# One denoising step of a hybrid backbone: residual kept in DRAM during the two networks, block products from the fifth pair on, some dots moved

## The chip, the cores and the metric

The kernel runs on one core of a Trainium2 chip. The core has a matrix engine (TensorE, "PE" in the profile; its weight loads are shown as "PEld"), a vector engine (VectorE, "DVE"), an activation engine (ScalarE, "ACT"), GpSimd ("POOL"), SyncE ("SP"), and 16 DMA engines that all issuing engines share. The metric is the device time of one execution in microseconds (us). The kernel before took 1848.61 us, the median of three runs from 1846.2 to 1849.77.

## The reference

One step of a backbone of two layers over 128 context tokens and 512 latent tokens, 1024 wide, all in float32:

```python
DEPTH = 2; D_MODEL = 1024; SEQ = 128; DEC_SEQ = 512; FFN_HIDDEN = 2816
for i in range(DEPTH):
    p_sh1, p_sc1, p_g1, p_sh2, p_sc2, p_g2 = modulation(c_ctx[None], mod_w[i], mod_b[i])
    s_sh1, s_sc1, s_g1, s_sh2, s_sc2, s_g2 = modulation(c, mod_w[i], mod_b[i])
    hp = modulate(xp, norm_mix_g[i], p_sh1, p_sc1)      # rmsnorm * (1 + scale) + shift
    hs = modulate(xs, norm_mix_g[i], s_sh1, s_sc1)
    op, os_ = mixer(hp), mixer(hs)                      # layer 0: two-way state scan; layer 1: attention
    xp = xp + p_g1 * op
    xs = xs + s_g1 * os_
    xp = xp + p_g2 * conv_ffn(modulate(xp, norm_ffn_g[i], p_sh2, p_sc2), *ffn_p)
    xs = xs + s_g2 * conv_ffn(modulate(xs, norm_ffn_g[i], s_sh2, s_sc2), *ffn_p)

def conv_ffn(h, up_w, conv_w, conv_b, down_w):
    u = dwconv(h @ up_w, conv_w, conv_b)                # 1024 -> 2 x 2816, width-3 convolution over tokens
    a, v = jnp.split(u, 2, axis=-1)
    return (jax.nn.silu(a) * v) @ down_w                # 2816 -> 1024

def modulation(cvec, w, b):
    m = jax.nn.silu(cvec) @ w + b                       # 1024 -> 6 x 1024
    return jnp.split(m[:, None, :], 6, axis=-1)
```

Each layer's `conv_ffn` is called a network here: the first network is that of layer 0, the second that of layer 1. The running `x` (640 tokens, 1024 wide) is the residual.

## The kernel before, in words

**Layout.** Features lie on the 128 partitions and all 640 tokens in the columns, so the residual is eight tiles of 128 x 640, `self.x[i]`. A float32 matrix product is made of three products of a faster format: every operand is split into a rounded part "hi" and the rest "lo", and hi·hi, hi·lo and lo·hi are added in PSUM. A block of 128 x 128 weights is so used three times, over two column ranges each (256 and 384, or 320 and 320): six matrix instructions.

**Stages.** The scan stage with its projection (`ssd`, L1131), the first network (`ffn`, L640, layer 0), the attention with its projection (`attention`, L1387), and the second network (`ffn`, layer 1). `stages` (L1496) and `run` (L1470) open and close memory pools around them.

**Order of the work.** The code is a straight list of instructions. A planner then sets the order on each engine from program order, readiness and an estimated cost of each instruction; every engine, and the queue of transfers that an engine issues, runs its list in that order. Side work is written as generators (`add`, L77): `hook` (L82), called after each weight block, advances a generator once as many ticks have passed as it asked for, and `drain` (L95) runs it to its end at that place of the program.

**Weights.** They come as "units" of up to 128 x 1024 in the order of use (`weight_units`, L1432). `prefetch` (L134) loads a unit from SP's queue into one of four "raw" slots. `cast` (L146) splits it: ACT writes hi, and lo is written either by DVE (raw - hi, L107) or, for the units in `self.summed`, by ACT (-hi) and an adding transfer of the weights from DRAM on POOL's queue (L181). `self.deep` says how many units ahead casts run (1, or 2 in the second network).

**The networks.** The 22 pairs of hidden tiles are made in stretches (`SUB`, L37), and after each stretch `project_out` (L321) multiplies the finished hidden tiles by the down weights, into eight output tiles. `gate_add` (L317) adds each PSUM result, times the gate, to the residual: DVE, three instructions per tile. The last stretch goes through `project_last` (L329), which also squares the new residual for the following norm. The first network has three stretches (8, 7, 7 pairs), the second five (4, 4, 4, 4, 6).

A pair in plain form is two tiles over eight weight blocks: 96 matrix instructions. From pair `S0[l]` on a pair is computed as a 2 x 2 block product with seven multiplications in place of eight, from sums of weights and sums of activations. `pair8` (L750), in the second network from pair 4, takes blocks of 4 + 4 weight blocks: 84 instructions of 320 columns. `pair7` (L782), in the first network from pair 16, takes 2 + 2 and does the remaining four plainly: 90. The sums of activations are made by `operands` (L688), those of weights in `cast`. `epilogue` (L657) does the convolution, SiLU and product on ACT and DVE, and splits the hidden tile; in the second network its lo is made by an adding transfer on POOL (L669). Both use the four slots "t" of 128 x 640 for temporary tiles.

**Memory.** The tag "f" has 19 slots of 128 x 640 for whatever is that size: the residual, scan inputs, raw tiles of the networks. The summed activations of the first network take over slots of the modulation work.

**Modulation of layer 1.** `mod_rest` (L598) makes 48 rows, each a 512 KB load and two dots (one for the latent tokens' vector, one for the context's) of 1024 columns on DVE (L620). All of it runs in the first network, as a generator that asks for 7 ticks, or 2 during a projection. It must end ahead of the stage that uses it.

**PSUM.** Up to the second network PSUM is a pool of three tiles of 1024 columns (`psd`); the second network uses six tiles of 512 (`psb`).

Of the kernel before, what the change touches and what calls it, by code (L numbers as in the profile page):

```python
# [18 lines left out]
P = 128  # L19
# [17 lines left out]
SUB = ((0, 8), (8, 15), (15, 22)), ((0, 4), (4, 8), (8, 12), (12, 16), (16, 22))  # L37
MIDS = 9, 6
# [3 lines left out]
NS = 2, 4  # L42
S0 = 16, 4
TH = T // 2
ATT_SPLIT = 6
NF = 19
# [3 lines left out]
class Step:  # L50


    def __init__(self, ctx, tc, a):
# [9 lines left out]
        self.down = False  # L63
# [7 lines left out]
        self.ph = pool("acts", 1)  # L71
        self.psb = None
# [42 lines left out]
    def slot(self, tag, name, dt=F32, cols=T, bufs=None, pool=None, rows=P):  # L115
        return (pool or self.ph).tile([rows, cols], dt, tag=tag, name=name, bufs=bufs)

# [203 lines left out]
    def project_out(self, h, ks, g, tiles=range(KT)):  # L321

        for i in tiles:
            ps = self.dense_ps("po")
            self.dense(ps, self.nextw(), ks, h)
            for hf in "AB":
                self.gate_add(i, ps, g, hf)

    def project_last(self, h, ks, g, nextnorm, ks_last=None, parts="AB"):  # L329
# [3 lines left out]
        for i in range(KT - 3):  # L333
# [6 lines left out]
            for hf in "AB":  # L340
                self.gate_add(i, ps, g, hf)
                self.norm_sq(i, hf)
        ks = ks_last or ks
        if self.modtask:
            self.drain(self.modtask)
        ws = [(self.dense_ps("po"), self.nextw(), i) for i in range(KT - 3, KT)]
        for hf in parts:
# [5 lines left out]
            self.normt[hf] = self.add(nextnorm(hf), 3)  # L353

# [85 lines left out]
    def first_tiles(self, h, pool):  # L440
# [70 lines left out]
        for i in range(KT):  # L511
            xi = self.slot("f", f"x{i}", bufs=NF)
# [85 lines left out]
    def mod_rest(self, l, t0, pool):  # L598


        nc, a = self.nc, self.a
        cb = pool.tile([P, 2, D], F32, tag="cbc", name="cbc", bufs=1)
        nc.sync.dma_start(cb, a["cbc"])
        for c in range(2):
            sb = self.pw.tile([P, 1024], F32, tag="raw", name="csil", bufs=RAW)
            self.act(sb, cb[:, c, :], AF.Tanh, scale=0.5)
            self.stt(cb[:, c, :], sb, 1.0, cb[:, c, :], ALU.add, ALU.mult)
            nc.vector.tensor_scalar(cb[:, c, :], cb[:, c, :], 0.5, None, ALU.mult)
        yield 4
        for t in range(t0 - 1, 48):  # L610
            if t < 47:
                nxt = pool.tile([P, 1024], F32, tag="mw", name="mw", bufs=2)
                nc.sync.dma_start(nxt, a["modT"][t + 1])
            if t < t0:
                w = nxt
                yield 8
                continue
            junk = self.slot("sq", "junk", BF16, cols=1024, bufs=1)
# [995 lines left out]
```

## Time and profile before

| | |
|---|---|
| median of three runs | 1848.61 us |
| profiled execution, its own time | 1847.95 us |
| its span, first to last instruction | 1846.2 us |
| granted TensorE clock, mean | 0.994 |
| instructions | 33204 |
| bytes moved | 230.28 MB |

The profile gives busy times by engine, a timeline in 40 slices, the DMA queues, the chain of work that ended last, and groups of instructions by source line (a helper's line, mostly: L101 any ACT instruction, L104 and L107 any DVE one, L110 any matrix product). Names such as `po<-mh,whi` are output and inputs: `up` the PSUM of the networks' pairs, `st` that of a stage's first three tiles, `po` that of a projection, `whi` and `wlo` the split weights, `mh` and `ml` the split hidden tile, `raw` a loaded unit, `uraw` a raw hidden tile, `xr` the residual, `mw` a modulation row, `ca`, `cv` the epilogue's temporary tiles. A group's row ends with its busy time, the mean of one in ns, and the idle time of the engine ahead of it with what ended it.

The execution runs through the stages in this order: the scan until about 480 us (its first projection is mixed with the scan's end), the scan's last projection to 559, the first network to about 1026, attention and its projections to about 1390, the second network to the end.

### The profile page before, as it was taken

The numbers are of one execution on the slowest core, as the hardware profiler recorded it, in microseconds if no ns is written. First come the engines' busy times: TensorE is split into PE (matmuls) and PEld (weight loads), VectorE is DVE, ScalarE is ACT, GpSimd is POOL, SyncE is SP. The second block draws the span as 40 slices with busy tenths as digits, with TensorE's granted clock in tenths as the row PEclk, the third lists the DMA queues.
The fourth block names the chain that finished last, engine by engine and source line by source line (L and its number), as shares of the span: only waits on it lengthen the run. The fifth ranks groups of instructions, "written<-read, shape, count | busy, mean of one in ns | idle before, by whom it ended". The sixth has DMA issues, their size and how long they took to land.

```text
span 1846.2 us, 33204 instructions
## 1 busy us (share of the span) xinstructions
PE 1802.7 (98%) x13070; PEld 1704.8 (92%) x13070; DVE 1490.5 (81%) x2969; ACT 1038.7 (56%) x1987; POOL 49.2 (3%) x60
## 2 busy tenths in 40 slices
PE   7999999999999999999999999999999999999997
PEld 5899999999989999999999988888899999999996
DVE  5689999999748999987585878777878877768784
ACT  3489686879326441343353556656636554746561
POOL 0000000000000000000000000000000010101110
PEclk9999999999999999999999999999999999999998
DMA  9844343445533556542122211211124445546451
GB/s 337 264 135 138 99 148 105 121 137 179 187 133 104 194 183 214 194 133 78 57 82 91 80 48 60 65 55 38 55 83 110 104 114 141 126 129 154 122 137 58
DMA packets 90051, 230.28 MB, mean 125 GB/s; under 512 B 10428, under 2 KB 17192, under 8 KB 89768
## 3 DMA queue, kind: packets, MB, share of 16 engines
q1 hardware_dynamic: 81256, 207.13, 34.8%
q0 software_dynamic: 8064, 20.52, 6.6%
q8 instruction: 102, 1.67, 0.4%
q10 hardware_dynamic: 576, 0.52, 0.1%
q14 instruction: 53, 0.43, 0.1%
HBM read 215.29 MB, written 5.96 MB: 120 GB/s over the span
## 4 chain that ended last, share of the span: by engine, by line
PE 86%; DVE 6%; ACT 3%; DMA 3%; issue 2%; SPq 0%; POOL 0%; DVEq 0%; POOLq 0%; ACTq 0%
PE up L110 27%; PE po L110 25%; PE z L110 6%; PE x L110 5%; PE st L110 5%; PE yp L110 3%; PE bc L110 3%; PE q L110 2%; PE k L110 1%; PE modrow L110 1%; PE sl L110 1%; ACT whi L101 1%; PE ov L110 1%; PE v L110 1%; ACT e L101 1%
## 5 line engine op out<-in xcount | busy, mean ns | idle before, releaser
L101 ACT ACTIVATE whi<-raw 128x1024 fp32r<-128x1024 f32 (+3 forms) x243 | 227.8, 939 | 277.3 <-PE po L110 167.4
L107 DVE TENSOR_TENSOR wlo<-raw,whi 128x1024 fp32r<-128x1024 f32 (+3 forms) x207 | 227.0, 1097 | 43.0 <-ACT whi L101 37.5
L104 DVE SCALAR_TENSOR_TENSOR xr<-po,mod,xr 128x256 f32<-128x256 f32 (+2 forms) x279 | 107.8, 432 | 108.9 <-PE po L110 108.8
L110 PE MATMUL po<-mh,whi 128*128 128x256 f32 (+1 forms) x704 | 166.9, 310 | 0.0
L110 PE MATMUL po<-ml,whi 128*128 128x256 f32 (+1 forms) x704 | 166.6, 309 | 0.0
L110 PE MATMUL po<-mh,wlo 128*128 128x256 f32 (+1 forms) x704 | 166.3, 309 | 0.0
L110 PE MATMUL up<-h01l,whi 128*128 128x256 f32 (+1 forms) x596 | 146.2, 308 | 0.0
L110 PE MATMUL up<-h01h,whi 128*128 128x256 f32 (+1 forms) x596 | 146.1, 310 | 0.1
L110 PE MATMUL up<-h01h,wlo 128*128 128x256 f32 (+1 forms) x596 | 145.6, 308 | 0.0
L110 PEld LDWEIGHTS po<-mh,whi 128*128 128x128 f32 x704 | 128.0, 188 | 0.7 <-ACT mh L101 0.5
L110 PEld LDWEIGHTS po<-ml,whi 128*128 128x128 f32 x704 | 128.2, 188 | 0.2 <-DVE ml L107 0.2
L110 PEld LDWEIGHTS po<-mh,wlo 128*128 128x128 f32 x704 | 128.2, 188 | 0.0
L110 PEld LDWEIGHTS up<-h01h,whi 128*128 128x128 f32 x596 | 108.9, 188 | 1.5 <-ACT uraw L101 1.1
L110 PEld LDWEIGHTS up<-h01l,whi 128*128 128x128 f32 x596 | 109.1, 188 | 0.0
L110 PEld LDWEIGHTS up<-h01h,wlo 128*128 128x128 f32 x596 | 109.0, 188 | 0.0
L110 PE MATMUL up<-h11h,whi 128*128 128x320 f32 (+1 forms) x368 | 107.3, 309 | 0.0
L110 PE MATMUL up<-h11l,whi 128*128 128x320 f32 (+1 forms) x368 | 107.2, 309 | 0.0
L110 PE MATMUL up<-h11h,wlo 128*128 128x320 f32 (+1 forms) x368 | 107.1, 309 | 0.0
L104 DVE SCALAR_TENSOR_TENSOR cv<-uraw,fcw,cv 128x511 f32<-128x511 f32 (+1 forms) x176 | 85.3, 545 | 14.8 <-ACT cv L101 14.8
L104 DVE SCALAR_TENSOR_TENSOR ca<-uraw,fcw,ca 128x127 f32<-128x127 f32 (+1 forms) x176 | 86.7, 545 | 8.8 <-ACT ca L101 7.5
L101 ACT ACTIVATE mh<-cv 128x640 fp32r<-128x640 f32 x44 | 32.5, 738 | 88.8 <-DVE cv L107 88.8
L101 ACT ACTIVATE whi<-s 128x512 fp32r<-128x512 f32 (+1 forms) x96 | 52.8, 571 | 52.2 <-DVE s L107 22.7
(531 smaller groups left out, 5074.4 us busy)
## 6 DMA issues: line engine op xcount, KB each, us to landing
raw<-in_w_up SPq DMA_DIRECT2D x88, 512.0 KB, 3.4
mw<-in_modT SPq DMA_DIRECT2D x48, 512.0 KB, 3.8
raw<-in_w_in SPq DMA_DIRECT2D x40, 512.0 KB, 5.5
rb<-rowd SPq DMA_DIRECT2D x40, 512.0 KB, 5.4
raw<-in_w_qkv SPq DMA_DIRECT2D x24, 512.0 KB, 3.3
mr<-in_mod SPq DMA_DIRECT2D x44, 256.0 KB, 5.2
wlo<-in_w_up POOLq DMA_DIRECT2D x17, 512.0 KB, 5.2
mp<-in_modp SPq DMA_DIRECT2D x32, 256.0 KB, 5.4
```

Source lines behind the costliest of these rows:

```text
L101: return self.nc.scalar.activation(out, in_, func, **k)
L104: return self.nc.vector.scalar_tensor_tensor(out, in0, s, in1, op0, op1)
L107: return self.nc.vector.tensor_tensor(out, a, b, op)
L110: return self.nc.tensor.matmul(out, lhsT, rhs, start=start, stop=stop, skip_group_check=more)
```

## The change

Seven things change together.

1. **Residual.** The residual gets a pool of its own (`xslot`, eight slots), which also serves the first eight scan inputs; "f" falls from 19 slots to 11. `project_last` of the scan and of the attention write each new residual tile to DRAM (`save`, SP). The pool is closed when a network has made its first tiles, and the sums of activations of that network take its place. `restore` opens it again ahead of the network's last projection and loads the eight tiles.
2. **Projections of the networks.** All but the last write gate times result into a tile y (ACT, three instructions per output tile), and a transfer on POOL's queue adds y to the residual in DRAM. y comes from the "t" slots in the first network, from three slots of its own in the second.
3. **First network like the second.** Five stretches, PSUM as `psb`, casts two units ahead, `pair8` from pair 4; `pair7` is removed.
4. **More adding transfers.** lo of hidden tiles in the first network; lo of most up weights of the first network; lo of ten of the sixteen units of the scan's output weights.
5. **Dots.** Rows 0 to 11 run in the scan's last projection, one dot every 2 ticks, with three row slots, and are drained ahead of its last three tiles. Rows 12 to 47 run in the first network, from 84 ticks after its start, one dot every 5 ticks.
6. **Pools.** The scan's pools are closed ahead of its last projection; PSUM pools are opened anew for each stage.
7. **Casts** run two units ahead in the scan's projections too.

```diff
-SUB = ((0, 8), (8, 15), (15, 22)), ((0, 4), (4, 8), (8, 12), (12, 16), (16, 22))
-MIDS = 9, 6
+SUB = (0, 4), (4, 8), (8, 12), (12, 16), (16, 22)
+MIDS = 6
-NS = 2, 4
-S0 = 16, 4
+NS = 4
+S0 = 4, 4
+EARLY = 12
-NF = 19
+NF = 11
+    def open_x(self):
+        self.xp = self.xctx.enter_context(self.tc.tile_pool(name="resid", bufs=1, side="right"))
+    def xslot(self, name):
+        return self.slot("x", name, bufs=KT, pool=self.xp)
+    def save(self, i):
+        if not self.xd:
+            self.xd = [self.dram.tile([P, T], F32, tag=f"xd{j}", name=f"xd{j}") for j in range(KT)]
+        self.nc.sync.dma_start(self.xd[i], self.x[i])
+    def restore(self):
+        self.open_x()
+        self.x = [self.xslot(f"xr{i}") for i in range(KT)]
+        for i in range(KT):
+            self.nc.sync.dma_start(self.x[i], self.xd[i])
...
+    def project_out(self, h, ks, g, tiles=range(KT), to=None):
...
+            y = to()
             for hf in "AB":
-                self.gate_add(i, ps, g, hf)
+                for a, b, c in COND[hf]:
+                    self.act(y[:, a:b], self.cols(ps, hf, a, b), AF.Copy, scale=g[:, i, c:c + 1])
+            self.nc.gpsimd.dma_start(self.xd[i], y, accum_op=ALU.add)
...
+            if save:
+                self.save(i)
         ks = ks_last or ks
-        if self.modtask:
-            self.drain(self.modtask)
+        for t in (self.modtask, *before):
+            if t:
+                self.drain(t)
...
+    def mod_rest(self, l, t0, t1, alloc, junk_, every):
...
-                yield 2 if self.down else 7
+                yield every
...
-            if l and p < FT - 1:
+            if p < FT - 1:
                 self.act(lo, cv, AF.Copy, scale=-1.0)
                 nc.gpsimd.dma_start(lo, cv, accum_op=ALU.add)
...
-        self.deep = 2 if l else 1
+        self.deep = 2
...
+        self.xctx.close()
+        with self.tc.tile_pool(name=f"sums{l}", bufs=1, side="right") as tp:
+            self.seven = self.add(operands(sevens, tp), 1)
+            for s, (k0, k1) in enumerate(SUB):
+                while done < min(k1 + 1, FT):
+                    pair(done, done + 1 < min(k1 + 1, FT))
+                    done += 1
+                if s < len(SUB) - 1:
+                    self.project_out(mid, range(k0, k1), self.gate(l, 1),
+                                     to=lambda: self.slot("y", "y", bufs=3, pool=pool) if l else self.tmp("y"))
+        if self.modtask:
+            self.drain(self.modtask)
+            self.modtask = None
+        self.restore()
+        self.project_last(mid, range(*SUB[-1]), self.gate(l, 1), nextnorm, parts="CD" if l else "AB")
...
+        self.deep = 2
         self.project_out(hy, range(8), self.gate(0, 0))
...
+        close()
+        self.open_mod()
+        with self.tc.tile_pool(name="po", bufs=1) as pool:
+            self.modtask = self.add(self.mod_rows(2, pool, 7))
+            row = lambda: pool.tile([P, 1024], F32, tag="ew", name="ew", bufs=3)
+            junk = lambda: self.slot("t", "junk", BF16, cols=1024, bufs=4)
+            early = self.add(self.mod_rest(1, 0, EARLY, row, junk, 2), 1)
+            self.project_last(hy, range(8), self.gate(0, 0), nextnorm, save=True, before=[early])
...
+        self.summed = (set(up) - set(up[:5]) - set(up[half:half + 5]) - after) | set(so[3:13])
...
+            self.modtask = self.add(self.mod_rest(1, EARLY, 48, self.mod_row, junk, 5), 84)
```

213 lines of the change are left out of this document (81 added, 132 removed).

## The prediction

> **What bounds the kernel now.** I read the page first, for the busy shares and the chain that ended last.
>
> ```profile
> span 1846.2 us, 33204 instructions
> PE 1802.7 (98%) x13070; PEld 1704.8 (92%) x13070; DVE 1490.5 (81%) x2969; ACT 1038.7 (56%) x1987; POOL 49.2 (3%) x60
> ...
> PE 86%; DVE 6%; ACT 3%; DMA 3%; issue 2%; SPq 0%; POOL 0%; DVEq 0%; POOLq 0%; ACTq 0%
> ```
>
> PE is busy for 98% of the span and carries 86% of the chain. So an edit gains only if it takes PE work away, and loses only if it makes PE wait. Second I cut the two networks into stretches. The columns are the stretch, its length, the busy time of PE, PEld, DVE, ACT and POOL, the granted clock, the DMA share and GB/s. The first five rows are the first network (products, projection, products, projection, products); the next five are the second network from its fifth tile on, in the same alternation; the last is the projection that ends the scan stage.
>
> ```profile
> 582.75:688.36 105.61, 105.61 (x722) 105.61 (x722) 105.44 (x181) 54.03 (x68) 0.00 (x0) 1.00 0.55 180
> 688.36:744.66 56.30, 56.30 (x386) 56.30 (x386) 55.92 (x100) 10.63 (x12) 0.00 (x0) 1.00 0.66 211
> 744.66:843.30 98.64, 98.64 (x675) 98.64 (x674) 86.44 (x149) 43.20 (x54) 0.00 (x0) 1.00 0.46 148
> 893.10:973.94 80.84, 80.75 (x542) 79.34 (x542) 66.42 (x133) 42.98 (x78) 0.00 (x0) 1.00 0.25 80
> ...
> 1412.79:1464.06 51.27, 49.48 (x327) 49.22 (x327) 43.27 (x83) 36.95 (x63) 8.00 (x9) 0.97 0.58 119
> 1464.06:1492.06 28.00, 28.00 (x195) 28.00 (x194) 20.50 (x44) 10.44 (x17) 1.73 (x2) 1.00 0.47 129
> 1492.06:1541.32 49.26, 49.26 (x339) 49.26 (x338) 37.86 (x71) 34.97 (x60) 7.87 (x9) 1.00 0.58 128
> 1541.32:1569.40 28.08, 28.08 (x195) 28.08 (x194) 20.61 (x44) 10.44 (x17) 1.74 (x2) 1.00 0.49 145
> 1569.40:1618.66 49.26, 49.26 (x339) 49.26 (x338) 37.74 (x71) 35.13 (x60) 7.87 (x9) 1.00 0.60 128
> 1723.86:1785.43 61.57, 61.57 (x422) 61.57 (x422) 49.60 (x91) 45.19 (x77) 10.46 (x12) 1.00 0.65 151
> 480.00:560.00 80.00, 80.00 (x585) 72.88 (x583) 47.15 (x96) 26.93 (x41) 0.00 (x0) 1.00 0.38 128
> ```
>
> In every one of them but the second network's opening, PE has no idle time worth naming. The chain gives the products' counts:
>
> ```profile
> 582.75 105.61 PE up L110 x720
> ...
> 744.66 98.63 PE up L110 x672
> ...
> 1492.06 49.26 PE up L110 x336
> 1541.32 28.08 PE po L110 x192
> ...
> 1785.43 6.25 PE po L110 x42
> ```
>
> 105.61/720, 98.63/672, 49.26/336 and 28.08/192 are all 146.6 ns a product (320 columns on average): the number of products is the time, in dense tiles and in block products alike.
>
> **The block products.** A dense pair is 2 tiles x 8 blocks x 3 terms x 2 halves = 96 products; pair7 has 90, pair8 has 84 (7 blocks of 4 x 3). The first network issues 16 dense pairs and 6 of pair7 now (2076), then 4 dense and 18 of pair8 (1896): 180 fewer, 26.4 us at 146.6 ns. I take the sum from whole stretches, since those hold the waits too. Now, from the fourth tile on: 105.61 + 98.64 + 80.84 = 285.1 us. The second network does exactly the work that the first will have: 51.27 (five dense tiles and the first pair8), three times 49.26 (four pair8 each) and 61.57 (five) = 260.6. Difference: 24.5 us less. This already holds the price of an early start: 324 products at 146.6 ns are 47.5 us of the 51.27, so building the summed operands beside the first epilogues costs 3.8 us of waiting. That wait is the bound from one side: without it the gain is 28.2 us. The projections keep 22 x 6 x 8 products however they are cut.
>
> **Dots.** 24 of the 96 dots move to the scan's projection; 72 stay.
>
> ```profile
> L620 DVE CUSTOM_DVE_ANT_0 mw<-mw,cbc 128x1024 f32<-128x1024 f32 x18 | 21.9, 1219 | 0.2
> ...
> L104 DVE SCALAR_TENSOR_TENSOR xr<-po,mod,xr 128x256 f32<-128x256 f32 x15 | 6.7, 479 | 6.3 <-PE po L110 6.3
> ...
> L104 DVE SCALAR_TENSOR_TENSOR xr<-po,mod,xr 128x128 f32<-128x128 f32 x7 | 2.4, 341 | 0.0
> ```
>
> 36 dots ran in the first stretch (this row and its twin), where the code's spacing of 7 ticks would have put about 14: the planner pulls them forward into every gap. That is why DVE stands at 105.44 of 105.61 there with PE unharmed, and why I charge dots only for what does not fit. After, four pairs and a projection take 49.3 + 28.1 = 77.4 us of PE. DVE owes 37.8 + 20.6, less the gate additions that go to ACT (6.7 + 2.4), plus 88 ticks' worth of dots (8.8 rows x 2 x 1.22 = 21.5): 70.8 of 77.4. It fits as a total. Within the products alone it would be 37.8 + 13.7 = 51.5 of 49.3; bound 0 to 2.2 us for each of some 4.5 stretches, and I take 0, because the full DVE above is the nearest row.
>
> In the scan's projection DVE is idle for 80.0 - 47.2 = 32.9 us, and gets back 5 x 1.22 from weight splits that become transfers: 39. It owes 24 x 1.22 = 29.3, and four instructions of that width for the SiLU, at most 4.9: 34. At 4 ticks a row, 8 rows fit the 40 ticks before the drain; 8 dots (9.8 us) are left ahead of the last three tiles' gate additions, on which the norm and the first network's start wait. Bound: 0 to 9.8. I take 2, since the idle time is there, but their rows must also arrive (next).
>
> **Transfers.** Shares and landings in a stretch of the second network, of the dot rows, and of the residual's load:
>
> ```profile
> q0 software_dynamic: 1403, 3.55, 42.6%
> q1 hardware_dynamic: 1185, 2.69, 17.1%
> ...
> mw<-in_modT SPq DMA_DIRECT2D x48, 512.0 KB, 3.8
> ...
> ml<-cv POOLq DMA_DIRECT2D x21, 320.0 KB, 4.2
> ...
> xr<-in_xT SPq DMA_DIRECT2D x8, 320.0 KB, 4.6
> ```
>
> In 49.3 us, accumulating transfers moved 3.55 MB in 21.0 us of the 16 engines (169 GB/s), plain ones 2.69 MB in 8.4 us (319 GB/s). The new y of 0.328 MB goes into DRAM with addition, which no row shows. At the plain rate it costs 1.03 us, at the accumulating rate 1.94; the destination is another memory, so twice that, 3.9, is my upper end. I take 1.94, the nearest operation. A projection of the second network then needs 0.49 x 28.1 = 13.8, plus 8 x 1.94 = 15.5: 29.3 of 28.1 us, with a stretch at 58% behind it to catch up. In the first network come 3.2 dot rows (0.524 MB at 319 GB/s, 1.64 us each): 34.5 of 28.1, 6.4 us too much; over the whole 77.4 us it is 28.6 + 13.8 + 15.5 + 14.5 = 72.4. So nothing is bound for good, but each of four projections runs a backlog of 6.4 us against buffers of four weight tiles and four "t" slots, 14 us of tiles. Bounds 0 and 25.6 in all; I take 6, because the densest row with PE full stands at 66% and this at 123%.
>
> In the scan's projection 0.38 x 80 = 30 us are used; 12 rows (19.7), the conditioning vectors (1.05 MB by the code, 3.3), eight saves (8.2) and five weight splits (5 x 0.524 MB at 169 GB/s, 15.5) make 77 of 80: this is the other ground of the 2 us above.
>
> **Smaller parts.** The y evacuations are 24 ACT instructions a projection in place of DVE's.
>
> ```profile
> 1400.83 0.37 ACT L101 ACTIVATE uraw<-st 128x256 f32<-128x256 f32 x1
> ...
> 1350.00 0.33 SPq L643 DMA_DIRECT2D fcw<-in_fcw  x1
> ...
> L669 POOL DMA_DIRECT2D ml<-cv x16: 864/867/885, 1513.6 to 1781.8; - x16
> ```
>
> 24 x 0.37 = 8.9 brings ACT from 10.4 to 19.3 of 28.1: hidden; three PSUM tiles cover a late one. POOL issues 8 more at 0.87 us in 28: hidden; while it waits for a y, the weight additions of the next products stand behind it, but the first weight after a projection is left to DVE. A y slot is held for 1.1 (ACT) + 0.9 + some 4.2 = 6.2 us; the second network's three slots give 10.5 us. SP's saves (0.33 us of issue each) make it wait for a gate addition, with weight loads behind; those were asked for four units earlier: 0. The reload before the last projection may start when the last summed operand is read, 24 products (3.5 us) before 1785.43; the first tile lands 4.9 us later, at 1786.9, and its gate addition is due 36 products after 1785.43, at 1790.7: hidden by 3.8 us, bound 0 to 1 a network. In the second network DVE was not the limit, so the additions taken from it gain nothing.
>
> **Sum.** The profiled execution took 1847.95 us (span 1846.2 and 1.75 around it), 0.7 under the median of 1848.61. 1847.95 - 24.5 + 6 + 2 = 1831.5, 1832 against the median.
>
> **Rivals.** *All of it hidden* (25%): backlogs stay in the buffers, and the first network's opening may even miss its 3.8 us. 1820 to 1827. For it: 99.8% DVE with PE full. Against: no stretch above has more than 66% of DMA. The Trainium skill, "DMA: Bandwidth & Descriptors", section on the anatomy of one SWDGE transfer, fits such a transfer as 2.0 us fixed plus bytes at 436 GB/s, so that a y would be an estimated 2.8 us of which 0.75 moves data; the first network's projection would then need 13.8 + 6.0 + 5.2 = 25.0 of 28.1, and this case would be the forecast. The rows here have 4.2 us for the same bytes into SBUF, so I do not follow it.
>
> *The additions into DRAM fill the DMA engines* (17%, the other side). Per 77.4 us the first network leaves 77.4 - 28.6 - 13.8 - 14.5 = 20.5 us for eight y, 2.6 each; the second 4.4 each. Every microsecond beyond 2.6 costs 32 us in four projections. At 3.4 us a y the gain of 24.5 is gone; that is where it decides. At my upper end of 3.9 it is 32 x 1.3 = 42: about 1866. For it: a read and a write of DRAM for each y, never seen here. Against: the adding row, 1.94. The same page, section "Issuing engines are not separate DMA queues", says that transfers from all issuers share the 16 engines and interleave; the window's 0.60 is indeed the sum of the two queues' 42.6% and 17.1%.
>
> *Dots in the way* (10%): the drained dots hold the norm before the first network for up to 9.8 us and the products lose 2.2 a stretch: 1831.5 + 7.8 + 4.5 x 2.2 = 1849 at worst, some 1841 in the middle. For it: DVE runs in order, and a dot whose row is late blocks it. Against: dots waited for a row 0.2 us in 18.
>
> *The change does not do what it says*, block products that wait at each block: excluded as far as 49.26 us for 336 products goes, with one difference, the dots between them; it is inside the case above.
>
> **Chances.** Forecast 48% (1827 to 1838), all hidden 25%, dots 10%, DRAM additions 17%. The range runs from 1819 to 1850, leaving out most of the last case. What this kernel's times can tell from no change is about 0.2%, 3.7 us. Faster 0.79, same 0.05, slower 0.16.
>
> **What would show it.** The first network's first tile starts now at
>
> ```profile
> 559.17 0.28 PE L110 MATMUL st<-h01h,whi 128*128 128x256 f32 x1
> ```
>
> Right: 180 fewer products in the first network, its stretches of four pair8 near 49.3 us and of five near 61.6, projections within 1 to 2 us of 28.1, a DMA share above 0.9 in them, a y landing in 5 to 8 us. Wrong: PE waiting for weights or for ACT's evacuation in the projections, y landings over 9 us, DVE idle on a dot's row, or more than the present 582.75 - 559.17 = 23.6 us from that tile's start to the end of the first three.

## The result, and the profile after

The changed kernel takes 1889.7 us (median of 4 runs, 1884.9 to 1890.6) against 1848.1: a ratio of 1.022 with a 95% interval of 1.020 to 1.024. It is slower by 41.6 us, where 16.5 us less were forecast. Its page begins, and gives the chain, so:

```profile
span 1887.5 us, 33747 instructions
...
PE 1796.7 (95%) x12890; PEld 1687.6 (89%) x12890; DVE 1470.3 (78%) x2919; ACT 1178.2 (62%) x2347; POOL 162.7 (9%) x190
...
PE 69%; DVE 14%; DMA 9%; ACT 5%; issue 4%; SPq 0%; POOL 0%; DVEq 0%; ACTq 0%; POOLq 0%
```

The 180 products are gone (13070 to 12890), but PE is busy for only 6 us less, where 180 products at 146.6 ns are 26: the mean granted clock fell from 0.994 to 0.984, and a product kept PE busy for 139.4 ns in the mean in place of 137.9. The span grew, PE's part of the chain fell from 86% to 69%, and that of DVE and DMA together rose from 9% to 23%: PE now waits. The timeline of the first three tiles of each stage gives the stages' starts (the last two numbers are the first and last start of a group). Before:

```profile
L110 PE MATMUL st<-h01h,whi x48: 276/332/386, 559.2 to 582.1; 128*128 128x256 f32 x24, 128*128 128x384 f32 x24
L110 PE MATMUL st<-h10h,whi x48: 274/334/386, 1025.6 to 1048.7; 128*128 128x256 f32 x24, 128*128 128x384 f32 x24
L110 PE MATMUL st<-h11h,whi x48: 280/334/386, 1390.1 to 1412.3; 128*128 128x256 f32 x24, 128*128 128x384 f32 x24
```

After:

```profile
L112 PE MATMUL st<-h01h,whi x48: 276/334/387, 587.1 to 609.5; 128*128 128x256 f32 x24, 128*128 128x384 f32 x24
L112 PE MATMUL st<-h10h,whi x48: 276/334/387, 1069.5 to 1091.6; 128*128 128x256 f32 x24, 128*128 128x384 f32 x24
L112 PE MATMUL st<-h11h,whi x48: 276/334/386, 1432.7 to 1455.1; 128*128 128x256 f32 x24, 128*128 128x384 f32 x24
```

The loss is in two places. The first network starts 27.9 us later (2 forecast), and takes 482.4 us in place of 466.4 (about 448 forecast: 24.5 less, 6 more). Attention and the second network are 1.3 us shorter each, less than these stages differ between kernels that leave them alone (below). 27.9 + 16.0 - 1.3 - 1.3 = 41.3, the difference of the spans.

**The scan's last projection.** Windows of it after the change (PE, PEld, DVE, ACT and POOL busy; granted clock, DMA share, GB/s):

```profile
500.00:520.00 20.00, 17.38 (x109) 12.10 (x108) 3.70 (x7) 5.66 (x7) 0.87 (x1) 1.00 1.03 331
520.00:540.00 20.00, 20.00 (x114) 13.35 (x113) 12.74 (x23) 2.86 (x5) 0.86 (x1) 1.00 1.04 380
540.00:560.00 20.00, 15.44 (x114) 13.92 (x112) 17.99 (x38) 5.10 (x9) 0.00 (x0) 0.99 0.67 237
560.00:570.00 10.00, 5.07 (x22) 4.77 (x22) 10.00 (x19) 0.00 (x0) 0.00 (x0) 0.50 0.62 200
```

and pieces of its chain (start, length, what; `ew` is a modulation row in this stage, `xr` a tile of the residual):

```profile
497.97 9.86 DMA mr<-in_mod
...
548.51 0.48 DVE xr L106
549.00 1.13 DVE ew L665
...
550.14 1.14 DVE junk L665
...
568.86 0.64 DVE ew L665
```

First the DMA engines are full for 40 us, with the loads of the projection's own modulation rows (mr) at their head. Their buffers are now in the pool that is opened in place of the scan's, so those loads could start only when the scan had ended: the first is issued at 494.5 us, against 446.6 in the kernel before. Then PE is half idle, while DVE works off 15 dots (14 of about 1.14 us on the chain and a part of the last, 16.7 us) between the gate additions (xr) on which the norm waits.

**The first network.** Three stretches of four pair8, the second and third projection between them (cut at whole microseconds), and waits of DVE, ACT and PE over the whole network (total us, times, longest; `s` is a sum of weights):

```profile
692.10:750.10 58.00, 51.40 (x330) 50.74 (x329) 52.60 (x100) 32.88 (x59) 8.91 (x11) 0.91 0.76 197
750.10:780.10 30.00, 29.32 (x197) 28.79 (x196) 23.39 (x42) 19.71 (x41) 7.86 (x9) 1.00 0.96 252
780.10:844.10 64.00, 51.36 (x328) 50.84 (x329) 53.33 (x99) 33.37 (x60) 8.71 (x10) 0.89 0.73 183
844.10:874.10 30.00, 29.35 (x202) 29.08 (x200) 24.68 (x46) 18.98 (x40) 7.83 (x9) 1.00 0.98 258
874.10:932.10 58.00, 52.23 (x331) 51.71 (x332) 45.91 (x86) 34.48 (x61) 8.73 (x10) 0.94 0.64 157
```

```profile
ACT whi L103 <- DVE s L109: 53.2, 19, 13.6
...
DVE junk L665 <- DMA mw<-in_modT: 32.3, 13, 4.7
...
PE up L112 <- ACT uraw L103: 15.6, 3, 11.6
...
PE up L112 <- DVE wlo L109: 9.1, 3, 4.4
```

The projections take 30 us, with PE busy for 29.3, at a DMA share of 0.96 to 0.98 (28.1 plus 1 to 2 were forecast); it is the products behind them that take 58, 64 and 58 us in place of 49.3. The chain from the end of a projection into the second of these stretches shows how:

```profile
766.72 10.21 DMA mw<-in_modT
...
776.95 1.23 DVE junk L665
...
779.96 7.97 DMA mw<-in_modT
...
787.95 1.22 DVE junk L665
...
790.48 6.25 DMA mw<-in_modT
...
796.75 1.22 DVE junk L665
...
797.99 0.62 DVE s L109
...
798.71 0.63 ACT whi L103
799.34 0.34 ACT uraw L103
...
799.72 0.64 PE up L112
```

A row's load waits for its slot, the row lands after 6 to 10 us, its dot runs, the next load starts. Behind the last dot on DVE stands the sum (s) that the next weight operand (whi) is made from; behind that operand on ACT stands the copy of a finished hidden tile out of PSUM (uraw); and for this copy PE waits, three times, for up to 11.6 us. The landings between 640 and 930 us, which holds the three cycles, from the window's DMA view (KB each, median us; `xd` is the residual in DRAM):

```profile
mw<-in_modT SPq DMA_DIRECT2D x32, 512.0 KB, 6.4
raw<-in_w_up SPq DMA_DIRECT2D x24, 512.0 KB, 7.1
xd<-y POOLq DMA_DIRECT2D x24, 320.0 KB, 8.2
```

### The profile page after: what moved, and what is told of

It is laid out like the page before. It is cut to its first block, busy times and chain, and to the rows that moved or that the text cites. A ratio compares the mean times of both kernels' runs of the same rounds, so it can differ in the third digit from the quotient of the medians.

```text
span 1887.5 us, 33747 instructions
## 1 busy us (share of the span) xinstructions
PE 1796.7 (95%) x12890; PEld 1687.6 (89%) x12890; DVE 1470.3 (78%) x2919; ACT 1178.2 (62%) x2347; POOL 162.7 (9%) x190
## 4 chain that ended last, share of the span: by engine, by line
PE 69%; DVE 14%; DMA 9%; ACT 5%; issue 4%; SPq 0%; POOL 0%; DVEq 0%; ACTq 0%; POOLq 0%
PE up L112 19%; PE po L112 17%; PE z L112 6%; PE x L112 5%; PE st L112 4%; DMA mw<-in_modT 3%; PE bc L112 3%; PE yp L112 3%; PE q L112 2%; DVE wlo L109 2%; ACT whi L103 2%; PE k L112 1%; PE modrow L112 1%; PE v L112 1%; DMA raw<-in_w_up 1%
## 5 line engine op out<-in xcount | busy, mean ns | idle before, releaser
L103 ACT ACTIVATE whi<-raw 128x1024 fp32r<-128x1024 f32 (+2 forms) x259 | 224.8, 869 | 196.6 <-PE po L112 103.8
L109 DVE TENSOR_TENSOR wlo<-raw,whi 128x1024 fp32r<-128x1024 f32 (+2 forms) x178 | 176.7, 993 | 53.3 <-ACT whi L103 52.3
L103 ACT ACTIVATE whi<-s 128x512 fp32r<-128x512 f32 x144 | 89.7, 627 | 103.9 <-DVE s L109 74.5
L109 DVE TENSOR_TENSOR wlo<-s,whi 128x512 fp32r<-128x512 f32 x144 | 98.0, 688 | 71.3 <-ACT whi L103 71.0
L112 PE MATMUL up<-Th,whi 128*128 128x320 f32 x432 | 136.4, 316 | 16.3 <-ACT uraw L103 16.3
L112 PE MATMUL up<-Tl,whi 128*128 128x320 f32 x432 | 135.9, 314 | 0.0
L112 PE MATMUL up<-Th,wlo 128*128 128x320 f32 x432 | 135.8, 314 | 0.0
L112 PE MATMUL up<-h01h,wlo 128*128 128x320 f32 (+1 forms) x368 | 110.0, 316 | 12.1 <-DVE wlo L109 9.1
L112 PE MATMUL up<-h01h,whi 128*128 128x320 f32 (+1 forms) x368 | 109.3, 315 | 2.1 <-ACT p L103 1.3
L112 PE MATMUL up<-h01l,whi 128*128 128x320 f32 (+1 forms) x368 | 109.1, 314 | 0.0
```

The costliest lines, as they stand in the source:

```text
L103: return self.nc.scalar.activation(out, in_, func, **k)
L109: return self.nc.vector.tensor_tensor(out, a, b, op)
L112: return self.nc.tensor.matmul(out, lhsT, rhs, start=start, stop=stop, skip_group_check=more)
```

## The experiments

All times by stage in one table, from the same rows of the timeline as above; the last columns are the median time and its ratio to the kernel before, with its 95% interval. The stage times are those of one execution of each kernel. The changed kernel and the ten whose scan is the same code start the first network at 584.7 to 589.5 us, and e7 and e8, with the same scan code too, at 569.8 and 576.6; attention, where nothing in it was edited, takes 361.7 to 366.6. So differences of 5 us or less between two rows are not taken as shown.

| kernel | first network starts | first network | attention | second network | us | ratio |
|---|---|---|---|---|---|---|
| before | 559.2 | 466.4 | 364.5 | 456.1 | 1848.1 | |
| after | 587.1 | 482.4 | 363.2 | 454.8 | 1889.7 | 1.022 (1.020 to 1.024) |
| e1 one row | 589.5 | 452.1 | 364.1 | 458.5 | 1865.7 | 1.010 (1.008 to 1.011) |
| e2 no additions | 586.1 | 458.3 | 361.7 | 456.2 | 1870.2 | 1.012 (1.009 to 1.014) |
| e3 no early rows | 570.1 | 482.6 | 364.2 | 458.2 | 1874.6 | 1.016 (1.012 to 1.020) |
| e4 open buffers | 564.9 | 491.4 | 364.2 | 457.2 | 1874.4 | 1.015 (1.013 to 1.017) |
| e5 neither | 588.5 | 445.5 | 362.6 | 455.3 | 1853.3 | 1.003 (1.002 to 1.004) |
| e6 three slots | 571.3 | 476.1 | 362.5 | 454.9 | 1867.9 | 1.010 (1.009 to 1.012) |
| e7 rows to attention | 569.8 | 472.3 | 372.3 | 456.8 | 1873.5 | 1.013 (1.012 to 1.015) |
| e8 half the rows | 576.6 | 467.8 | 377.7 | 455.0 | 1875.1 | 1.014 (1.011 to 1.017) |
| e9 held | 586.9 | 483.0 | 363.3 | 454.6 | 1889.0 | 1.021 (1.019 to 1.023) |
| e10 held, all 48 | 561.1 | 504.9 | 366.6 | 458.0 | 1889.9 | 1.020 (1.017 to 1.024) |
| e11 rows unread | 584.7 | 482.9 | 364.5 | 454.7 | 1891.8 | 1.024 (1.022 to 1.025) |
| e12 plain y | 586.0 | 468.0 | 364.3 | 454.8 | 1878.2 | 1.017 (1.015 to 1.019) |
| e13 held, one row | 588.8 | 467.3 | 362.6 | 456.3 | 1873.6 | 1.014 (1.012 to 1.015) |
| e14 held by 12 | 589.2 | 477.7 | 364.2 | 456.2 | 1887.0 | 1.020 (1.018 to 1.022) |
| e15 held by 24 | 588.0 | 455.9 | 363.1 | 456.7 | 1866.7 | 1.010 (1.009 to 1.012) |
| e16 scan as before | 561.3 | 483.1 | 364.2 | 454.1 | 1865.2 | 1.009 (1.008 to 1.010) |
| e17 rows 40 and 8 | 563.5 | 465.9 | 362.7 | 465.4 | 1858.9 | 1.006 (1.005 to 1.007) |
| e18 held by 36 | 588.1 | 469.7 | 363.6 | 455.1 | 1874.6 | 1.014 (1.012 to 1.016) |

### The scan's last projection

**e3: no early rows.**

```diff
+        if t0 == 0:
+            nc.vector.memset(self.mod[l][:, 0:t1, :], 0.5)
+            return
         for t in range(t0 - 1, t1):
```

> Rows 0 to 11 are left out of the scan's projection, loads and 24 dots (a constant stands in their place in the second layer's modulation); the SiLU of the conditioning vectors stays, and the scan's buffers are still closed ahead of the projection. In the changed kernel the first network starts at 588.6 us, before it started at 559.2. Theory C (24 dots bunched ahead of the last three tiles' gate additions): it starts at 562 to 570, the whole is 1863 to 1873. Theory D (the projection's own modulation rows can only be loaded once the scan's buffers are closed, and PE waits for them): it starts at 578 to 587, the whole is 1879 to 1889.

The start comes 17.0 us earlier, at 570.1, the edge of theory C's 562 to 570: the dots, with the loads of their rows, are the larger part, but the rest is not theirs.

**e4: the scan's buffers open.**

```diff
-        close()
-        self.open_mod()
-        with self.tc.tile_pool(name="po", bufs=1) as pool:
-            self.modtask = self.add(self.mod_rows(2, pool, 7))
-            ...
-            self.project_last(hy, ..., save=True, before=[early])
+        self.modtask = self.add(self.mod_rows(2, pool, 7))
+        self.project_last(hy, range(8), self.gate(0, 0), nextnorm, save=True)
+        close()
+        self.open_mod()
```

The lines left out here put a constant in place of the 12 rows and move the SiLU of the conditioning vectors into the first network.

> As in the kernel without rows 0 to 11 (24 dots and 12 loads left out, a constant in their place), and besides the scan's buffers stay open during its last projection, so that the first layer's modulation rows can be loaded ahead of it as before; the SiLU of the conditioning vectors moves to the first network's start. Theory D: the first network starts at 559 to 563 us, that is 15 to 25 us earlier than with the buffers closed. Theory C: it starts within 5 us of the run with the buffers closed. On both, the first network keeps its 481 us or a little more.

Another 5.2 us, far from the 15 to 25 of theory D and at the edge of C's 5. The first network became 8.8 us longer (491.4 against 482.6), and the whole stayed where it was (1874.4 and 1874.6). In e10, e16 and e17, whose scan differs from this one chiefly in that DVE splits the weights again in place of adding transfers, the start is 561.1, 561.3 and 563.5: 1.4 to 3.8 us for the splits. So of 27.9 us, 17.0 are the drained dots and their rows; some 5 for the closed buffers and 1 to 4 for the splits by transfers fit the rows of the table but are too small to be shown by them, and no run looks at the last 2.

### The first network: which of its parts costs

**e1: one row.** The load inside the loop is left out from the second row on, and both dots of a row write to junk, so that the one row stays as it is.

```diff
-            if t < t1 - 1:
+            if t < t1 - 1 and (t0 == 0 or t < t0):
                 nxt = alloc()
                 nc.sync.dma_start(nxt, a["modT"][t + 1])
```

> The 72 dots of the first network all read the one row that is loaded ahead of them; the other 35 row loads (0.524 MB each) are left out, so the modulation of the second layer is not the right one. The dots stay, with their 1.22 us each. In the changed kernel the first network lasts about 481 us from its first tile to attention's, where 442 were forecast. Theory A (a dot whose row is late holds DVE, which runs in order, and PE ends up waiting): the first network falls to 440 to 452 us, the whole to 1848 to 1862. Theory B (DVE is simply too full in the products, or the evacuations and additions of y cost it, with or without rows): the first network stays at 474 to 482, the whole at 1880 to 1890.

**e2: no additions.**

```diff
-            self.nc.gpsimd.dma_start(self.xd[i], y, accum_op=ALU.add)
+            if self.add_y:      # the second network alone
+                self.nc.gpsimd.dma_start(self.xd[i], y, accum_op=ALU.add)
```

> The 32 transfers that add a y to the residual in DRAM are left out in the first network only (the residual lacks four of its five stretches there); ACT's evacuations of y, the dots and their row loads stay. Theory A1 (the additions into DRAM fill the DMA engines, and that is why rows are late): rows land in about 4 us as before, DVE's idle time on rows goes from 32 us to under 10, the first network falls by 25 to 40 us, the whole is 1848 to 1865. Theory A2 (rows are late because a row is loaded only one row ahead, into two slots, behind other traffic that is there anyway): the first network falls by less than 12 us, the whole stays above 1876.

**e5: both edits in one kernel.**

> Both edits of the first network together: 35 row loads left out (all dots read one row) and the 32 additions of y left out; the modulation of the second layer and the residual are incomplete. Dots and evacuations keep their instructions. The first network was 482 us in the changed kernel, 452 without the rows, 458 without the additions, and 442 was forecast. Theory E (what is left of the loss without rows, 10 us, is what the additions do to the weights' loads and splits): 440 to 446 us. Theory F (it is the dots' own time on DVE and ACT's evacuations): 449 to 453.

452.1 us without row loads (theory A), 458.3 without additions (just short of A1's 25 us, far from A2's 12), 445.5 without either (theory E), 482.4 with both. In e1 up to 7 dots stand within 10 us, more than the 5 of the changed kernel, and with their row at hand they cost little. In e2 rows land after 5.2 us in the median in place of 6.4, and DVE waits for them for 13.4 us in place of 32.3: the additions are a part of why rows are late.

From the lowest, the additions alone cost 6.6 us, the rows alone 12.8, the two together 36.9: more than the sum. How much more isn't settled. e2's trace is of the fastest of its four executions, 6 us under their median; by the medians of the whole kernel the three are 12.4, 16.8 and 36.4, and the excess over the sum is 7 us in place of 17. Without either, one cycle of products and projection reads:

```profile
692.50:740.50 48.00, 48.00 (x329) 48.00 (x329) 47.91 (x91) 33.57 (x61) 7.84 (x9) 1.00 0.57 127
740.50:770.50 30.00, 30.00 (x208) 30.00 (x208) 29.81 (x55) 19.86 (x41) 1.76 (x2) 1.00 0.45 127
```

DVE is busy for 77.7 of 78 us, and PE for all of them. So the dots themselves harm little so long as none waits; a dot that does wait finds, in such a cycle, no gap on DVE in which the lost time could be made up.

**e12: y written, not added.**

```diff
-            self.nc.gpsimd.dma_start(self.xd[i], y, accum_op=ALU.add)
+            self.nc.gpsimd.dma_start(self.xd[i], y, **({'accum_op': ALU.add} if self.add_y else {}))
```

> In the first network each y is written to the residual's place in DRAM in place of being added to it, from the same queue and with the same bytes; the residual is lost there. Rows and dots stay. Without these transfers the first network took 458 us, with them 482. If it is the addition that costs (two accesses to DRAM for each byte, 1.94 us of 16 engines in place of about 1.03): 464 to 470 us. If it is any transfer of that size in the queue: 476 to 482.

468.0 us, as expected of the addition: of the 24 us that the 32 transfers cost in these traces, 14 are the addition, 10 the transfer itself.

### The first network: late rows, or too many transfers

**e6: three slots**, on e4, with rows loaded two ahead; `NF = 10`.

```diff
-        return self.mp.tile([P, 1024], F32, tag="mw", name="mw", bufs=2)
+        return self.mp.tile([P, 1024], F32, tag="mw", name="mw", bufs=3)
```

> The kernel with the scan's buffers open and without rows 0 to 11, and in the first network three slots for rows in place of two, each row loaded two rows ahead; the space comes from one slot fewer for loose operands (10 in place of 11) and from closing the conditioning's buffers earlier. With two slots the first network took 491 us. Theory G (a row is late because its slot comes free too late; the bandwidth is there): DVE's idle time on rows falls from 30 us to under 10, the first network takes 455 to 472 us, the whole is 1838 to 1856. Theory H (the DMA engines are full, so that a deeper queue of rows only moves the lateness to the weights): the first network stays above 480, the whole above 1862.

**e7: rows 36 to 47 in attention; e8: rows 24 to 47.** Both with three slots and no rows in the scan.

```diff
+            row = lambda: self.pw.tile([P, 1024], F32, tag="raw", name="mw", bufs=RAW)
+            rest = self.add(self.mod_rest(1, 36, 48, row, junk, 7, 1), 20)
```

> All 48 rows are done, but not in the scan's projection: rows 0 to 35 in the first network with three slots, rows 36 to 47 in attention, through the weights' load buffers; the scan's buffers stay open during its last projection. Theory G: the first network starts at 562 to 566 us and takes 455 to 475, attention 363 to 372 in place of 364, the whole is 1840 to 1862. Theory H: the first network stays above 480, the whole above 1865.

> As the kernel before it in this list, with rows 0 to 23 in the first network (48 dots in place of 72, spaced by 7 ticks) and rows 24 to 47 in attention (48 dots, 58 us more of DVE, which has 78 us idle there). Theory G: the first network takes 448 to 460 us; attention costs 0 to 15 us more; the whole is 1828 to 1850. Rival (attention's chain of waits is tight on DVE, and each dot delays it): attention takes 385 us or more, and the whole is above 1855.

The third slot gave 15.3 us of the 19 to 36 expected (491.4 to 476.1) and settled nothing between the two theories. DVE's waits for rows fell from 30.2 us (e4) to 13.7, but PE's waits for the copies out of PSUM hardly did (19.3 to 16.6): with three slots late rows are not all that holds the sums up, and what does is open. The start came later, 569.8 to 576.6 in the three kernels against 564.9, with one slot fewer for operands. Attention pays for dots: 8 us for 24, 13 for 48, though DVE has idle time there. With 24 rows in place of 36, a third fewer and 7 ticks apart, e8's first network is 4.5 and 8.3 us shorter than in e7 and e6; above e1's 452.1 it keeps 15.7 us of their 20.2 and 24.0.

**e9: each dot held at its written place.**

```diff
+                dot = nc.vector.tensor_tensor_reduce(...)
+                if t0 > 0:
+                    self.hold(dot, [self.last])    # the product written just before
```

> The changed kernel with one addition: each of the first network's 72 dots waits for the product that was written just ahead of it, so that the planner can't pull it forward. Rows, additions, slots and all other work stay. In the changed kernel's trace the dots stand in clumps in and behind the projections (3 to 4.5 in 10 us, up to 20 us into the next products) and none or one in the second half of the products; the projections are where the additions of y load the DMA engines. Theory I (the pulled-forward clumps are what waits: rows in the projections land late, and the sums for the next weights stand behind the dots on DVE): the first network falls from 482 us to 452 to 466, the whole to 1858 to 1873. Theory H (the transfers are simply too many, wherever the dots stand): it stays above 474, the whole above 1880.

**e10: the same for all 48 rows, the scan as in e4 with its weights split by DVE.**

> All 48 rows in the first network with two slots and 96 dots held at their places, 4 ticks apart; none in the scan's projection, whose buffers stay open and whose weights are split by DVE as in the kernel before. Theory I: the first network starts at 559 to 563 us and takes 458 to 476 (24 dots more than in the run with 72 held ones), the whole is 1838 to 1858. Rival (DVE has no room for 96 dots at fixed places in these networks): the first network takes over 480, the whole over 1862.

**e11: rows loaded and not read.**

```diff
-tensor_tensor_reduce(w if c else junk, w, cb[c], ...
+tensor_tensor_reduce(w if c and not t0 else junk, cb[0] if t0 else w, cb[c], ...
```

> The changed kernel with all 36 row loads of the first network kept, but its 72 dots read a conditioning vector that is there anyway in place of their row, so that no dot waits for a load and no load for a dot; the second layer's modulation is not the right one. Theory J (DVE, which runs in order, is held by dots whose rows are late; the traffic alone does little): the first network falls from 482 us to 450 to 460 (452 with the loads left out as well), the whole to 1856 to 1868. Theory H (the rows' traffic, beside the additions, makes every other load and split late, whoever waits for a row): it stays at 470 to 482, the whole above 1875.

Three misses: e9 and e11 came out on the side of theory H (483.0 and 482.9), e10 on that of its rival (504.9). By themselves they would be the end of theory I. But in e9 and e11 the kernel lost its time in a new place. In e11 nothing paced the loads any more, they ran ahead into the opening, and from the first tile to the end of the first projection it took 132 us in place of 105 (read from windows of 1 us), with ACT waiting for a projection weight for up to 22.1 us; the three stretches after that took 55, 51 and 48, with the same loads under way, where the changed kernel takes 58, 64 and 58. In e9 no dot waits for a row; instead DVE waits for the products that dots are held behind, and PE for adding transfers. These land as fast as in the changed kernel (after 4.9 us in the median for `ml` and 6.5 to 6.6 for `wlo`, against 5.1 and 6.1 to 6.7), which leaves a late issue:

```profile
PE up L112 <- DMA wlo<-in_w_up: 14.2, 6, 4.5
DVE mw L666 <- PE up L112: 13.6, 5, 5.9
PE po L112 <- DMA ml<-cv: 12.9, 4, 5.2
DVE junk L666 <- PE po L112: 10.9, 6, 3.0
DVE junk L666 <- PE up L112: 8.4, 6, 2.3
DVE mw L666 <- PE po L112: 6.6, 4, 2.6
```

39.5 us of DVE's time went into the hold (the four rows of DVE). The next runs measure that.

**e13: e9 and e1 together.**

> Dots held at their written places and all reading the one resident row (35 row loads left out, the modulation of the second layer not the right one): what holding costs by itself. In the run with held dots and their rows, DVE waited 33 us for the products that its dots were held behind, and the first network stayed at 483 us. Theory H (transfers): without the row loads the first network falls to 450 to 458, as it did without holding (452). Theory K (a held dot stops DVE, which otherwise works ahead of PE, and so costs what it saves): it stays at 468 to 483.

467.3, between the two theories: the hold alone costs 15.2 us (452.1 without it), and rows another 15.7.

**e14, e15, e18: held behind the product 12, 24 and 36 ticks ahead.**

```diff
+        self.marks.append(self.last)                # in hook(), once a tick
...
+                    self.hold(dot, [self.marks[-24]])
```

> The changed kernel; each of the first network's dots waits for the product written 12 ticks (some 10 us) ahead of its place, so that DVE may run ahead by that much and the clumps are cut down. Theory K with rows as the cause (clumps wait for late rows; a loose hold spreads them without stopping DVE): the first network takes 455 to 470 us, the whole 1860 to 1876. Theory H: it stays at 476 to 484, the whole above 1881.

> The same with 24 ticks (some 21 us). Theory K: between the kernel with 12 ticks and the changed kernel's 482 us. Theory H: no difference, 476 to 484.

> The changed kernel with each dot of the first network held behind the product 36 ticks (some 32 us) ahead of its place. Held by 24 ticks the first network took 456 us, by 12 ticks 478, not held 482. If the order of DVE decides by and by (the hold only has to cut off the clumps): 456 to 475. If the value at 24 ticks was an accident of one order: 476 to 484.

Not held 482.4, by 36 ticks 469.7, by 24 455.9, by 12 477.7, at the place 483.0. e14 came out as theory H had it, e15 as neither theory had it (12 ticks should have been the better one), and e18 in the range for an order that decides by and by. The five values make one curve, which DVE's waits explain: for rows it waits 32.3 us with no hold and 24.6, 16.8, 9.0 and 0.0 as the hold gets tighter, for the products that dots are held behind 0.0, 13.6, 14.5, 33.2 and 39.5. Each value is one order of DVE's work, and that 24 is the best place, rather than a good one, isn't shown. With the same dots and transfers as the changed kernel, the first network is 26.5 us shorter there (the whole 23.0, by the medians), and PE's wait for the copies out of PSUM (15.6 us) is gone. Its stretches, and the chain over the first of them:

```profile
691.00:739.00 48.00, 48.00 (x329) 47.93 (x328) 43.64 (x83) 33.76 (x61) 8.93 (x11) 1.00 0.79 191
739.00:768.00 29.00, 29.00 (x202) 28.92 (x200) 23.59 (x43) 19.27 (x39) 7.10 (x9) 1.00 0.94 252
768.00:819.00 51.00, 49.08 (x333) 48.63 (x332) 45.90 (x86) 34.05 (x62) 9.52 (x11) 1.00 0.82 199
```

```profile
690.65 49.39 PE up L114 x336
```

336 products in 49.39 us, as forecast, next to a projection at a DMA share of 0.94. Its landings in the window of 640 to 930 us are much like the changed kernel's: 6.9 us in the median for rows (6.4 there), 6.2 for up weights (7.1), 7.6 for a y (8.2).

So these transfers can be borne (theory H falls as the whole cause), and rows may land late: what costs is a dot that waits for its row in front of the sums on a full DVE. The 10.4 us that e15 stays above e5 are the rest, transfers and hold together.

### Both stages together

**e16 and e17**: the scan of e10, dots held by 24 ticks. e16 has 48 rows in the first network, 4 ticks apart; e17 has 40, 5 ticks apart, and the last 8 in the second network's opening.

> All 48 rows in the first network, 4 ticks apart, each dot held behind the product 24 ticks ahead of its place; no rows in the scan's projection, its buffers open, its weights split by DVE. From the runs so far: the first network starts at 561 us (as with the dots at their exact places), takes 456 us plus 24 dots more (29 us of DVE, 12 rows of traffic): 458 to 480; the whole is 1836 to 1860. If the gain of the loose hold was an accident of that one order, the first network takes over 485.

> As the kernel before it in this list, but rows 40 to 47 (the last gate) go to the second network's first products, with the conditioning vectors loaded and prepared again there; 40 rows stay in the first network, 5 ticks apart. The first network starts at 561 us and takes 456 to 470; the second network takes 455 to 465; the whole is 1836 to 1855.

The scan's part came back in both (561.3, 563.5). e16's first network misses its range by 3. The 27.2 us that it is longer than e15's are near what 24 further dots take on DVE (29.3), but its waits tell another story:

```profile
DVE junk L670 <- DMA mw<-in_modT: 36.0, 15, 5.8
...
PE up L115 <- ACT uraw L106: 15.7, 3, 8.0
```

These are the changed kernel's waits again, and DVE waits for the products that dots are held behind for only 0.2 us (14.5 in e15): with 96 dots, 4 ticks apart, a hold of 24 ticks no longer holds anything. e17's first network takes 465.9, but its second network pays 9 to 11 us for 16 dots and a second preparation of the vectors. At 1858.9 us it is the fastest with all 48 rows and all additions, and still 0.6% slower than the kernel before. No version faster than that kernel was found.

## Why the prediction was wrong

*Block products, -24.5: right.* 180 fewer products, 49.39 us for 336 of them, and 445.5 us for a first network without rows' loads and additions, where 466.4 - 24.5 = 441.9 was expected.

*The price of a y: right.* In the first projection after the last dot, the adding queue moved

```profile
q0 software_dynamic: 1063, 2.39, 53.5%
```

in 28.08 us (seven y, one hidden tile, one weight split): 15.0 us for 2.39 MB, 2.06 us for the bytes of a y (1.94 taken), and the projection kept its 28.08 us. The rival of additions that fill the DMA engines, which needed 3.4 us to eat the gain, falls with it as it was put; that the additions make rows late (e2) is another matter. The Trainium skill, "DMA: Bandwidth & Descriptors", section on the anatomy of one SWDGE transfer, would have a y landed in an estimated 2.8 us; the changed kernel's trace has a median of 8.2 in the loaded cycles, just over the 5 to 8 forecast. The section describes one transfer, and none here is alone.

*Transfers, +6, and dots in the products, 0: the step that failed in the first network.* The two were priced one by one, and each price was near. The backlog was there as worked out (share 0.96 to 0.98), and the dots fit as a total (77.7 of 78 us in e5). What was left out is what late transfers do to the dots. The backlog was weighed "against buffers of four weight tiles and four 't' slots, 14 us of tiles"; the rows' two slots were not in that list. With landings of 6 to 10 us, dot and load take turns, DVE stands behind the dot, the weight sums behind DVE, and ACT's copies out of PSUM behind the sums. So the three stretches of products lost 8.7, 14.7 and 8.7 us, where dots were given 0 to 2.2 a stretch and 0 was taken "because the full DVE above is the nearest row": in that row the dots' rows landed after 3.8 us. The loss was 36.9 us (482.4 - 445.5), over the bound of 25.6 for transfers, because that bound counted backlog in projections and the loss came in the products behind them. That rows and additions act through this wait is what e1, e2 and e15 show; the part of the transfers that reaches PE by other ways (e6, and the 10.4 us left in e15) stays open.

*The scan's projection, +2: wrong by 26.* The drained dots were sized at 9.8 at most and cost 17.0, their rows included: the conditioning vectors were issued at 508.5 us, behind 16 of the late loads, so the first dot began at 522.6, and 15 of them, not 8, were left ahead of the last gate additions. That closing the scan's buffers moves those loads behind the scan's end (some 5 us) wasn't in the working at all, though the list of changes names it. Splits by adding transfers (1 to 4 us) were costed as DMA time only. Five of them fall in the time after 480 us, as costed; the nine from 440 us on land after 8.1 us in the median:

```profile
wlo<-in_w_so POOLq DMA_DIRECT2D x9, 512.0 KB, 8.1
```

*The rivals.* "Dots in the way" (10%) named the cause in both places, down to "a dot whose row is late blocks it", and was too small by far (1849 at worst). Its sign, DVE idle on a dot's row, came up with 32.3 us. The evidence held against it, dots that waited 0.2 us in 18, came from a trace in which rows land in 3.8 us; the change itself raised that to 6.4.

*Smaller parts: right as far as seen.* Attention and the second network lost nothing that the spread between traces would show.

## What to carry to other kernels

When a change adds traffic, reprice every load that an in-order engine waits for at the new landing time, and compare that with the smallest prefetch it has (here two slots), not with the largest. An engine that is full without harm is a reason for care: it has little to make up a wait with. Work that a planner may pull forward can want a loose bound, some 20 us here: in this kernel none and a tight one were both worse, and with a third more dots (e16) the same bound did nothing.

## What the runs showed of the hardware

- Where PE waited long, its products ran longer as well. The first network of the changed kernel and that of e5 have the same products:

```profile
587.10:1069.50 482.40, 449.80 (x3037) 445.03 (x3033) 386.27 (x741) 294.21 (x538) 76.78 (x88) 0.96 0.72 183
588.50:1034.00 445.50, 439.89 (x3040) 436.78 (x3032) 385.71 (x741) 293.56 (x538) 48.78 (x56) 1.00 0.53 133
```

  The granted clock was 0.96 against 1.00, and PE was busy for 9.9 us more: of the 36.9 us between the two, some 27 are waiting and 10 are longer products. Waits that add up to 11 us, none over 3.0 (e1), went with a clock of 1.00; what sets the clock isn't separated by these runs.
- Two kinds of transfers that cost 6.6 and 12.8 us alone (12.4 and 16.8 by the medians) cost 36.9 (36.4) together, in stretches with a DMA share of 0.64 to 0.98.
- A y that is added in DRAM landed after 8.2 us in the median in the loaded cycles, one that is only written (e12) after 5.7.
